# A two-layer conditioned decoder trunk: the list scheduler orders its instructions with a timeline model of the machine

## The chip, the cores and the metric

The kernel runs on one core of a Trainium2 chip. The metric is the device time of one execution in microseconds (us), the median of three runs.

## What is computed

The reference is a trunk of two post-norm layers on one sequence of 256 tokens with 1024 features, in float32. Each layer has three sub-layers: a SwiGLU feed-forward network (FFN, inner width 2816), a mixer, and a second FFN. Layer 0 mixes with a gated linear recurrence (RG-LRU) and chunked gated linear attention side by side, layer 1 with multi-head latent attention. A conditioning vector `c` gives shift, scale and gate vectors for each sub-layer, and each sub-layer ends in a layer norm over the residual sum:

```
for l in range(DEPTH):
    mod = c_act @ mod_w[l] + mod_b[l]
    sh1, sc1, g1, sh2, sc2, g2, sh3, sc3, g3 = jnp.split(mod, N_MOD, axis=-1)
    f = swiglu(modulate(x, sh1, sc1), ffn_in[l, 0], ffn_out[l, 0])
    x = deepnorm_residual(x, f, g1, ln_g[l, 0], ln_b[l, 0], 0.5)
    u = modulate(x, sh2, sc2)
...
    x = deepnorm_residual(x, m, g2, ln_g[l, 1], ln_b[l, 1])
    f = swiglu(modulate(x, sh3, sc3), ffn_in[l, 1], ffn_out[l, 1])
    x = deepnorm_residual(x, f, g3, ln_g[l, 2], ln_b[l, 2], 0.5)
```

Here `deepnorm_residual` is `layer_norm(DN_ALPHA * x + weight * (1 + gate) * f)`, and `m` is the mixer's output.

## The kernel before

**Layout.** Activations are kept transposed: features on the 128 partitions, the 256 tokens on the free axis, so that a vector of 1024 features is 8 tiles of 128x256. A weight block of 128x128 is loaded into TensorE (PE) and a tile of activations is streamed past it.

**Weights.** The weights arrive in the order in which they are used, as slabs of 1 MB (16 blocks), by transfers that SyncE (SP) issues into the buffers `wraw`. To keep float32 accuracy each half slab is split in two parts: ScalarE (ACT) makes the high part `whi` at L354, VectorE (DVE) the low part `wlo` at L355, five buffers each. The activations are split in the same way into `uhi` and `ulo` (or `hhi` and `hlo` inside an FFN). Each block then takes three matmuls: L432 (high by high), L433 (low activations by high weights) and L434 (high activations by low weights), in `mm3`.

**Modulation.** The matrix `mod_w` comes in slabs too, through the same `wraw` buffers and the same SP queue. DVE reduces 144 of its blocks with the conditioning vector (L406). A table of targets sets how many reduces are due at each slab of weights; they are spread over the whole kernel, ahead of where their vectors are needed.

**An FFN.** In `ffn`, the first passes go over groups of output tiles with the feature tile k outside, so that they need `u(k)` one by one. ACT applies SiLU, DVE multiplies (L772), and the product is split by ACT (L479) and DVE (L480). Where the first passes cover only part of the features, ACT keeps the partial sums and DVE adds them at L817. Then come the output matmuls.

**A boundary between sub-layers** (class `Boundary`). DVE makes the residual sum of each output tile at L648, adds to running sums (L655, L656), and scales the unnormalised tile into `flat` (ACT L620, DVE L621). Behind the last tile, `stats` runs four matmuls with a matrix of ones: L664 and L666 sum to the mean, L665 and L667 to the mean of squares. ACT squares the mean (L675), DVE takes the variance (L681) and subtracts the mean from each of the 8 tiles (L670, `center`), and `rsqrt2` gives the inverse deviation `r` (ACT L454, DVE L756 and L757). While that goes on, PE runs "early" matmuls: the first blocks of the next sub-layer's weights on the unnormalised tiles, whose result is corrected afterwards (ACT L707, DVE L709 and L710). They are 48 matmuls at the boundary that the prediction shows, accumulators `mm_4864` and `mm_4904`. `u(k)` then gives the normalised, modulated tile: DVE L725 makes `ut`, ACT L728 the high part `uhi`, DVE L729 the low part `ulo`. `residual` makes the input of the next residual sum: DVE L735 (`xh`, three buffers) and ACT L736, 8 of each; it is needed only at the end of the sub-layer.

**What sets the order.** The code above is a program in source order. The tile framework's list scheduler turns it into one queue for each engine, which the engine then runs strictly in order; semaphores make an instruction wait for its operands and its buffers. The scheduler picks among the instructions that it holds to be ready by priority. The code raises priorities (`tc.high_priority`, with an offset of 100 for `u(k)`, of 60 for the corrections of the early tiles, and the default for the boundary), fixes the order of a few stretches (`tc.manual_schedule`), and adds edges without semaphores between single instructions (`queue_behind`). What it holds to be ready, and when, is its model's matter.

The function that the change touches:

## Time and profile before

| quantity | value |
|---|---|
| runs (us) | 1019.43, 1019.33, 1018.88; median 1019.33 |
| profiled execution (us) | 1018.88, its span 1017.2 |
| PE, DVE, ACT busy (us) | 996.6, 876.8, 611.4 |
| DMA | 258.56 MB, mean 254 GB/s |
| granted PE clock, mean | 0.997 |

A busy time is the time in which an engine has an instruction in work. An engine's line in the timeline gives the start, the duration, the engine, the source line, the operation, the tiles (result on the left of the arrow) and their shape; a bracket behind it tells how long the engine was idle just before, and what it waited for. Durations overlap: an engine takes the next instruction before the last one has ended, so the price of an instruction in a full queue is the distance from its start to the next start.

### The profile page before, as it was taken

What the parts mean: (1) busy time and instruction counts of PE and PEld (TensorE: products, weight loads), DVE (VectorE), ACT (ScalarE), POOL (GpSimd) and SP (SyncE); (2) the same over time, 40 slices, a digit from 0 to 9 for tenths busy, and PEclk for the clock granted to TensorE, in tenths of its full rate; (3) what the DMA queues carried; (4) which work ended last, traced back from release to release, by engine and by line L of the source; (5) the groups of instructions that cost most, each with busy time, mean ns of one, the idle gap of its engine ahead of it and who ended that gap; (6) DMA issues with size and microseconds to landing.
All of it is one profiled execution on the core that took longest, in us unless ns stands there. A gap on an engine that the chain in (4) does not pass through costs nothing.

```text
span 1017.2 us, 20534 instructions
## 1 busy us (share of the span) xinstructions
PE 996.6 (98%) x8344; PEld 976.4 (96%) x8344; DVE 876.8 (86%) x1503; ACT 611.4 (60%) x1021; POOL 6.7 (1%) x27
## 2 busy tenths in 40 slices
PE   9999999999999999999999999999999999999995
PEld 7999999998999999999999999999999899999995
DVE  5789999798999999999987899999788799667664
ACT  4756665578896766655555664454568776454542
POOL 0000000000000000000000000000000000000000
PEclk9999999999999999999999999999999999999998
DMA  9997798554467954799986479898743146766501
GB/s 346 417 380 297 279 354 319 223 203 174 159 252 297 355 198 172 273 375 398 338 296 246 166 261 385 325 338 320 277 166 125 54 178 237 268 225 242 193 16 42
DMA packets 38145, 258.56 MB, mean 254 GB/s; under 512 B 4241, under 2 KB 5777, under 8 KB 7714
## 3 DMA queue, kind: packets, MB, share of 16 engines
q1 hardware_dynamic: 38050, 257.25, 67.4%
q8 instruction: 65, 1.06, 0.4%
q14 instruction: 30, 0.25, 0.1%
HBM read 256.18 MB, written 1.05 MB: 253 GB/s over the span
## 4 chain that ended last, share of the span: by engine, by line
PE 81%; DVE 15%; issue 2%; ACT 2%; DMA 1%; DVEq 0%; ACTq 0%
PE mm L433 23%; PE mm L432 23%; PE mm L434 23%; DVE wlo L355 5%; DVE junk L406 3%; PE mm L795 2%; PE mm L1074 1%; PE mm L1073 1%; DMA wraw<-modw 1%; PE mm L1075 1%; PE ax L795 1%; DVE flat L817 0%; DVE flat L941 0%; DVE ax L636 0%; DVE h L772 0%
## 5 line engine op out<-in xcount | busy, mean ns | idle before, releaser
L355 DVE TENSOR_TENSOR wlo<-wraw,whi 128x1024 fp32r<-128x1024 f32 x338 | 411.5, 1225 | 74.6 <-ACT whi L354 74.2
L354 ACT ACTIVATE whi<-wraw 128x1024 fp32r<-128x1024 f32 x338 | 355.4, 1058 | 186.2 <-PE mm L433 147.7
L432 PE MATMUL mm<-uhi,whi 128*128 128x256 f32 x1624 | 449.2, 277 | 1.3 <-ACT sg L454 1.3
L433 PE MATMUL mm<-ulo,whi 128*128 128x256 f32 x1624 | 449.5, 277 | 0.2 <-DVE ulo L729 0.2
L434 PE MATMUL mm<-uhi,wlo 128*128 128x256 f32 x1624 | 449.2, 277 | 0.0
L432 PEld LDWEIGHTS mm<-uhi,whi 128*128 128x128 f32 x1624 | 304.4, 188 | 1.7 <-ACT sg L454 1.5
L433 PEld LDWEIGHTS mm<-ulo,whi 128*128 128x128 f32 x1624 | 305.0, 188 | 0.7 <-DVE ulo L729 0.4
L434 PEld LDWEIGHTS mm<-uhi,wlo 128*128 128x128 f32 x1624 | 305.0, 188 | 0.1
L434 PE MATMUL mm<-hhi,wlo 128*128 128x256 f32 x704 | 194.7, 277 | 1.1 <-DVE wlo L355 1.1
L433 PE MATMUL mm<-hlo,whi 128*128 128x256 f32 x704 | 194.6, 276 | 0.0
L432 PE MATMUL mm<-hhi,whi 128*128 128x256 f32 x704 | 194.6, 276 | 0.0
L406 DVE CUSTOM_DVE_ANT_0 junk<-wraw,cact,cols 128x1024 bf16<-128x1024 f32 x136 | 174.9, 1286 | 7.9 <-DMA wraw<-modw 7.0
L434 PEld LDWEIGHTS mm<-hhi,wlo 128*128 128x128 f32 x704 | 132.2, 188 | 1.3 <-DVE wlo L355 1.3
L433 PEld LDWEIGHTS mm<-hlo,whi 128*128 128x128 f32 x704 | 132.2, 188 | 0.0
L432 PEld LDWEIGHTS mm<-hhi,whi 128*128 128x128 f32 x704 | 132.2, 188 | 0.0
L479 ACT ACTIVATE hhi<-h 128x256 fp32r<-128x256 f32 x88 | 35.7, 414 | 60.2 <-DVE h L772 60.0
L652 ACT ACTIVATE ysq<-yy 128x256 f32<-128x256 f32 x42 | 17.5, 416 | 43.8 <-DVE yy L648 41.0
L772 DVE SCALAR_TENSOR_TENSOR h<-mm,sg 128x256 f32<-128x256 f32 x75 | 31.6, 427 | 7.8 <-PE mm L434 7.5
L480 DVE TENSOR_TENSOR hlo<-h,hhi 128x256 fp32r<-128x256 f32 x88 | 36.7, 426 | 0.2 <-ACT hhi L479 0.2
L648 DVE SCALAR_TENSOR_TENSOR yy<-mm,gate,ax 128x256 f32<-128x256 f32 x48 | 23.2, 482 | 15.2 <-PE mm L434 15.2
L454 ACT ACTIVATE sg<-mm 128x256 f32<-128x256 f32 x75 | 27.4, 367 | 6.8 <-PE mm L434 4.8
L432 PE MATMUL mm<-flat,whi 128*128 128x258 f32 x96 | 28.5, 297 | 0.0
(310 smaller groups left out, 1117.5 us busy)
## 6 DMA issues: line engine op xcount, KB each, us to landing
wraw<-wst SPq DMA_DIRECT2D x165, 1024.0 KB, 5.6
wraw<-modw SPq DMA_DIRECT2D x71, 1024.0 KB, 7.1
wraw<-wst SPq DMA_DIRECT2D x10, 512.0 KB, 9.9
wraw<-modw SPq DMA_DIRECT2D x2, 512.0 KB, 5.3
yy<-xT SPq DMA_DIRECT2D x8, 128.0 KB, 10.2
wraw<-rgw SPq DMA_DIRECT2D x1, 1024.0 KB, 4.8
outT<-yy SPq DMA_DIRECT2D x3, 256.0 KB, 2.5
outT<-yy SPq DMA_DIRECT2D x2, 128.0 KB, 2.1
```

The lines of the kernel that those rows point to most:

```text
L354: ia = act.activation(hi, raw, AF.Copy)
L355: i = vec.tensor_tensor(lo, raw, hi.bitcast(F32), SUB)
L406: i = vec.tensor_tensor_reduce(junk, t, cact, 1.0, bias, MULT, ADD, self.modcols[(l, v)][:, j:j + 1])
L432: pe.matmul(ps, hi, mh, start=start, stop=False, skip_group_check=shared)
L433: pe.matmul(ps, hi, ml, start=False, stop=False, skip_group_check=shared)
L434: pe.matmul(ps, lo, mh, start=False, stop=stop, skip_group_check=shared)
L454: i = act.activation(out, in_, func, **kw)
L479: act.activation(hi, src, AF.Copy)
L480: return vec.tensor_tensor(lo, src, hi.bitcast(F32), SUB)
L648: vec.scalar_tensor_tensor(y, ps, self.gate[:, f:f + 1], ax[:, f, :], MULT, ADD)
L772: vec.scalar_tensor_tensor(h, pu, bu, sg, ADD, MULT)
L795: pe.matmul(grp[j][:, half * SEQ:(half + 1) * SEQ], wt[w], mv, start=k == ks[0] and half == 0 and t == 0, stop=k == ks[-1] and t == len(te ...
```

## The change

One argument is given to the context in which the program is recorded:

```
-    with _tile.TileContext(nc) as tc:
+    with _tile.TileContext(nc, schedule_with_timeline_sim=True) as tc:
         trunk_kernel(tc, *args)
```

With it the scheduler decides by a timeline model of the machine, and no longer by its plain one, when an instruction is ready and which comes next. The sources of the operations, their priorities, the fixed stretches and the added edges stay. The same instructions come out, in another order: 1345 lines of the order differ on PE, 1956 on DVE, 1033 on ACT, 24 on SP and 11 on GpSimd.

Here is what DVE's queue holds at the end of layer 0's mixer, behind the statistics. `v_4843` is the variance, `yy_4208` the 8 residual sums, `ut_4860` and `ut_4987` belong to `u(0)` and `u(1)`, and `wlo` are low parts of weights. Before:

```order
L681 TENSOR_TENSOR v_4843<-ax_4836,v_4843 128x256
L670 TENSOR_TENSOR yy_4208<-yy_4208,ax_4835 128x256 x4
L756 SCALAR_TENSOR_TENSOR t_4853<-v_4843,t_4853 128x256
L670 TENSOR_TENSOR yy_4208<-yy_4208,ax_4835 128x256
L757 SCALAR_TENSOR_TENSOR r_4852<-t_4853,r_4852 128x256
L670 TENSOR_TENSOR yy_4208<-yy_4208,ax_4835 128x256
L725 SCALAR_TENSOR_TENSOR ut_4860<-yy_4208,hA_4231,r_4852 128x256
L709 SCALAR_TENSOR_TENSOR early_4901<-mean_4845,wab_4899,mm_4864 128x256
L725 SCALAR_TENSOR_TENSOR ut_4987<-yy_4208,hA_4231,r_4852 128x256
L729 SCALAR_TENSOR_TENSOR ulo_138<-ut_4860,B_4223,uhi_137 128x256
```

Now DVE's queue has, from L681 on, all eight L670, two L709, L756, L757, and two each of L725 and L710, and then these rows, in which `junk` is a modulation reduce and `xh` a residual step:

```order
L355 TENSOR_TENSOR wlo_4868<-wraw_4576,whi_4867 128x1024
L355 TENSOR_TENSOR wlo_4872<-wraw_4576,whi_4871 128x1024
L355 TENSOR_TENSOR wlo_4910<-wraw_4662,whi_4909 128x1024
L355 TENSOR_TENSOR wlo_4960<-wraw_4662,whi_4959 128x1024
L406 ISA junk_5136,mod_8_817_5135<-wraw_4905,cact_96,cols_97 128x1024
L406 ISA mod_8_817_5135 128x1
L735 SCALAR_TENSOR_TENSOR xh_5262<-yy_4208,ag_4227,r_4852 128x256
L735 SCALAR_TENSOR_TENSOR xh_5265<-yy_4208,ag_4227,r_4852 128x256
L735 SCALAR_TENSOR_TENSOR xh_5268<-yy_4208,ag_4227,r_4852 128x256
L729 SCALAR_TENSOR_TENSOR ulo_138<-ut_4860,B_4223,uhi_137 128x256
```

The first L729 has moved from the 12th instruction behind L681 to the 26th (repeats and the read of the accumulator counted), behind four weight conversions, a reduce and three residual steps.

On PE at the same place, the statistics stood ahead of the early matmuls, whose first blocks follow. `mm_4864` is an early accumulator:

```order
L664 MATMUL ax_4835<-acc_4209,ones_dm_98 128x256
L665 MATMUL ax_4836<-acc_4209,ones_dm_98 128x256
L666 MATMUL ax_4835<-yy_4208,ones_dm_98 128x256
L432 MATMUL mm_4864<-flat_692_4233,whi_4699 128x258
L667 MATMUL ax_4836<-ysq_4831,ones_dm_98 128x256
L433 MATMUL mm_4864<-flat_693_4234,whi_4699 128x258
L434 MATMUL mm_4864<-flat_692_4233,wlo_4700 128x258
```

Now they stand behind the early matmuls, and the first matmuls on `u(0)`, with accumulators `mm_4955` to `mm_4958`, follow at once:

```order
L434 MATMUL mm_4864<-flat_692_4233,wlo_4700 128x258
L433 MATMUL mm_4904<-flat_693_4234,whi_4736 128x258
L434 MATMUL mm_4904<-flat_692_4233,wlo_4737 128x258
L664 MATMUL ax_4835<-acc_4209,ones_dm_98 128x256
L666 MATMUL ax_4835<-yy_4208,ones_dm_98 128x256
L665 MATMUL ax_4836<-acc_4209,ones_dm_98 128x256
L667 MATMUL ax_4836<-ysq_4831,ones_dm_98 128x256
L432 MATMUL mm_4955<-uhi_137,whi_4802 128x256
L432 MATMUL mm_4956<-uhi_137,whi_4802 128x256
L432 MATMUL mm_4957<-uhi_137,whi_4802 128x256
L432 MATMUL mm_4958<-uhi_137,whi_4802 128x256
L433 MATMUL mm_4955<-ulo_138,whi_4802 128x256
```

The last early matmul has moved from some 5.5 us of PE work behind L667 to ahead of it, and the first L432 on `u(0)` from behind the early matmuls to right behind L667.

At the end of layer 0, on the way to the first FFN of layer 1, DVE's queue now holds this around the first two `ulo` (`ut_7259` and `ut_7379` are those of `u(0)` and `u(1)`):

```order
L725 SCALAR_TENSOR_TENSOR ut_7259<-yy_6486,hA_6497,r_7251 128x256
L710 SCALAR_TENSOR_TENSOR early_7294<-early_7294,r_7251 128x256
L725 SCALAR_TENSOR_TENSOR ut_7379<-yy_6486,hA_6497,r_7251 128x256
L355 TENSOR_TENSOR wlo_7352<-wraw_7075,whi_7351 128x1024
L709 SCALAR_TENSOR_TENSOR early_7332<-mean_7244,wab_7330,mm_7297 128x256
L735 SCALAR_TENSOR_TENSOR xh_7653<-yy_6486,ag_6493,r_7251 128x256
L735 SCALAR_TENSOR_TENSOR xh_7656<-yy_6486,ag_6493,r_7251 128x256
L735 SCALAR_TENSOR_TENSOR xh_7659<-yy_6486,ag_6493,r_7251 128x256
L406 ISA junk_7529,mod_3_1089_6816<-wraw_7298,cact_96,cols_97 128x1024
L406 ISA mod_3_1089_6816 128x1
L504 TENSOR_SCALAR v_8876<-v_8876,cols_97 128x256
L729 SCALAR_TENSOR_TENSOR ulo_138<-ut_7259,B_6489,uhi_137 128x256
```

In before, that first L729 stands behind L681 with five L670, L756, L757, one L355, two L725 and one L709 between; now residual steps, two reduces and three L355 stand there as well.

## Prediction

> **What bounds the kernel now.** I read the page first: its head, the busy times, the chain that ended last.

> ```profile
> span 1017.2 us, 20534 instructions
> PE 996.6 (98%) x8344; PEld 976.4 (96%) x8344; DVE 876.8 (86%) x1503; ACT 611.4 (60%) x1021; POOL 6.7 (1%) x27
> PE 81%; DVE 15%; issue 2%; ACT 2%; DMA 1%; DVEq 0%; ACTq 0%
> ```

> PE has work in 98% of the span, and the chain runs through it for 81% and through DVE for 15%. So the kernel has almost no slack on PE, and any new PE idle time is paid in full, while DVE at 86% can hide a reordering only where it has a lead. How tight that is, the waits of PE tell (us in total, times, longest):

> ```profile
> PE ax L1130 <- DVE B L601: 1.7, 1, 1.7
> PE mm L432 <- ACT sg L454: 1.3, 1, 1.3
> PE mm L434 <- DVE wlo L355: 1.1, 1, 1.1
> PE mm L433 <- DVE ulo L729: 0.2, 1, 0.2
> ```

> The largest single wait is 1.7 us, and the matmuls that need the low part of the normalised activations (ulo, L729) wait 0.2 us in the whole run. That last row is the one that the change will move. Next I read the timeline at one sub-layer boundary, from the mixer of layer 0 to its second FFN. PE first (start, us, engine, line, operation):

> ```profile
> 375.78 0.28 PE L432 MATMUL mm<-uhi,whi 128*128 128x256 f32 x1
> ...
> 380.43 0.28 PE L434 MATMUL mm<-uhi,wlo 128*128 128x256 f32 x1
> ...
> 382.24 0.60 PE L667 MATMUL ax<-ysq,ones_dm 128*128 128x256 f32 x2
> ...
> 388.31 0.28 PE L432 MATMUL mm<-uhi,whi 128*128 128x256 f32 x1
> ```

> The first two rows are 41 matmuls apart: 4.65 us, so 0.1133 us from start to start. That is the price of a matmul here. L667 finishes the statistics at 382.84. The first matmul that needs the normalised activations (L432 on uhi) starts at 388.31. In the 5.5 us between, PE runs the early matmuls on the unnormalised activations (flat), without a gap. DVE in the same time:

> ```profile
> 382.94 0.42 DVE L681 TENSOR_TENSOR v<-ax,v 128x256 f32<-128x256 f32 x1
> 383.28 1.41 DVE L670 TENSOR_TENSOR yy<-yy,ax 128x256 f32<-128x256 f32 x4
> ...
> 385.93 0.48 DVE L725 SCALAR_TENSOR_TENSOR ut<-yy,hA,r 128x256 f32<-128x256 f32 x1
> 386.83 0.48 DVE L709 SCALAR_TENSOR_TENSOR early<-mean,wab,mm 128x256 f32<-128x256 f32 x1 [0.41 <-ACT wab L707]
> 387.23 0.48 DVE L725 SCALAR_TENSOR_TENSOR ut<-yy,hA,r 128x256 f32<-128x256 f32 x1
> 387.62 0.48 DVE L729 SCALAR_TENSOR_TENSOR ulo<-ut,B,uhi 128x256 fp32r<-128x256 f32 x1
> 388.02 0.42 DVE L710 SCALAR_TENSOR_TENSOR early<-early,r 128x256 f32<-128x256 f32 x1
> 388.35 0.48 DVE L729 SCALAR_TENSOR_TENSOR ulo<-ut,B,uhi 128x256 fp32r<-128x256 f32 x1
> 388.75 2.35 DVE L355 TENSOR_TENSOR wlo<-wraw,whi 128x1024 fp32r<-128x1024 f32 x2
> 391.02 0.48 DVE L709 SCALAR_TENSOR_TENSOR early<-mean,wab,mm 128x256 f32<-128x256 f32 x1
> ```

> L681 starts 0.10 us after L667's end and the first ulo is done at 388.10, 0.3 us ahead of its matmul: the early matmuls cover this chain almost exactly. The same rows price DVE's work, from start to start. L681 is 0.34. The eight operations from 383.28 to 385.93 (six L670, L756, L757) are 0.33 each, L710 too. L709, L725 and L729 are 0.40, and L355 is 1.135 (two in 2.27). Further prices, from later in the same FFN:

> ```profile
> 405.84 1.28 DVE L406 CUSTOM_DVE_ANT_0 junk<-wraw,cact,cols 128x1024 bf16<-128x1024 f32 x1
> 407.04 0.08 DVE L406 DVE_READ_ACCUMULATOR2_ANT mod<- 128x1 f32 x1
> ...
> 409.38 0.48 DVE L735 SCALAR_TENSOR_TENSOR xh<-yy,ag,r 128x256 f32<-128x256 f32 x1
> 409.78 0.42 DVE L772 SCALAR_TENSOR_TENSOR h<-mm,sg 128x256 f32<-128x256 f32 x1
> 410.12 1.22 DVE L355 TENSOR_TENSOR wlo<-wraw,whi 128x1024 fp32r<-128x1024 f32 x1
> ...
> 411.58 0.42 DVE L480 TENSOR_TENSOR hlo<-h,hhi 128x256 fp32r<-128x256 f32 x1
> 411.91 1.28 DVE L406 CUSTOM_DVE_ANT_0 junk<-wraw,cact,cols 128x1024 bf16<-128x1024 f32 x1
> ```

> So a modulation reduce (L406) is 1.20, a residual step (L735) 0.40, L772 and L480 0.33 each. In before, the first L735 of this FFN runs at 409.38 and the first reduce at 405.84, more than 20 us behind the statistics.

> **The change part by part.** No instruction is added or removed; each engine runs the same work in another order. In order queues that costs nothing except where a loop closes: a PE instruction that DVE waits for, a block of DVE work queued behind it, and a later PE instruction that waits for the end of that block. If the DVE block is longer than the PE work between the two, PE must idle for the difference, whatever else happens. I looked for such blocks along the two orders, with the prices above. The waits that they give in before are those that the rows of waits show; after has seven of another size.

> *Boundaries.* The new order places the statistics L664 to L667 behind the early matmuls, so that L432/L433 on u follow L667 at once: the cover of 5.5 us is gone, since it now lies ahead of the chain and not beside it. And DVE's queue ahead of ulo is longer: all eight L670, residual steps L735, reduces L406 and weight conversions L355 stand there. At the boundary shown above, DVE has from L681 to the fifth L729: L681 0.34, 8 L670 2.64, L756 and L757 0.66, 2 L709 0.80, 6 L725 2.40, 2 L710 0.66, 7 L355 7.95, 5 L406 6.00, 8 L735 3.20, 5 L729 2.00, L772, L480 and two small ones 0.80. The sum is 27.45. Between L667 and the L433 that waits for that L729, PE has 102 matmuls, 11.56. The difference, 15.9, is PE idle time; 13 of it comes at the first L433. The other boundaries by the same prices:
> - layer 0, first FFN to mixer: 8 L670, 3 L355, 2 L709, 2 L725 and five others, 9.4, against 30 matmuls, 3.4: 6.0.
> - layer 0 to layer 1: 8 L670, 6 L355, 6 L406, 8 L735, 6 L725, 5 L729 and others with 1.6 of rope tables, 29.0, against 128 matmuls, 14.5: 14.5.
> - layer 1, first FFN to attention: 8 L670, 8 L735, 5 L355, 4 L709, 4 L710 and others, 16.5, against 74 matmuls and three of two passes, 9.7: 6.8.
> - layer 1, attention to second FFN: 8 L670, 8 L735, 3 L355, 2 L406, 4 L725, 3 L729 and others, 16.8, against 52 matmuls, 5.9: 10.9.

> Together 54.1. Before waits a few tenths at each (0.2 at ulo, above); less 0.3 each, 1.5, that is 52.6.

> *Two long blocks.* In the first FFN and in layer 0's mixer DVE is full already. Windows of before (us, PE busy, PEld, DVE, ACT, POOL, clock, DMA share, GB/s):

> ```profile
> 97.00:142.00 45.00, 43.69 (x385) 43.49 (x385) 45.00 (x78) 31.03 (x49) 0.00 (x0) 1.00 0.84 315
> ...
> 259.00:303.00 44.00, 42.94 (x328) 41.04 (x328) 42.98 (x70) 38.00 (x77) 0.00 (x0) 1.00 0.56 207
> ```

> The timeline prices what else is in the mixer's block, the chain what is in the FFN's:

> ```profile
> 258.44 0.69 DVE L932 TENSOR_SCALAR ya<-ya 128x1024 f32<-128x1024 f32 x1
> 259.04 0.48 DVE L735 SCALAR_TENSOR_TENSOR xh<-yy,ag,r 128x256 f32<-128x256 f32 x1
> 259.44 1.22 DVE L933 SCALAR_TENSOR_TENSOR ya<-ya,ya 128x1024 f32<-128x1024 f32 x1
> 260.57 0.42 DVE L1055 TENSOR_TENSOR bc<-bc,mm 128x256 f32<-128x256 f32 x1
> ...
> 267.51 2.44 DVE L941 TENSOR_TENSOR_SCAN flat<-ya,ya 128x256 f32<-128x256 f32 x4
> ```

> ```profile
> 104.61 0.60 DVE flat L817
> ```

> In the first FFN 16 L355, 15 L406, 14 L772, 14 L480 and 7 L817 (0.60) now lie in one loop: 18.2 + 18.0 + 4.6 + 4.6 + 4.2 and 0.3 of small ones are 49.9. Its 390 matmuls take 45.6 at the window's own pace (385 in 45.0): 4.3 more. In the mixer 12 L406, 12 L355, 12 L921 (0.40, an operation of L725's kind and size), 6 L735, 4 L941 (0.61), four wide ones of 1.13 and two of 0.60, with 5.1 of small ones, come to 48.5 against the 44.0 that the window took for nearly the same PE work: 4.5 more.

> *Smaller terms.* The first FFN's block also needs a modulation slab whose transfer is now queued behind a conversion that ends 4.2 us before its reduce.

> ```profile
> wraw<-modw SPq DMA_DIRECT2D x71, 1024.0 KB, 7.1
> ```

> By the median landing that is 7.1 − 4.2 = 2.9 more, between 0 and 7. Two ACT conversions (L354, 1.06 by the group's mean) now stand ahead of ACT's part of the statistics at two boundaries: between 0 and 2.1 each, and I take 0.7, since ACT had idle time just ahead; 1.4. ACT's tanh chain in the mixer closes a loop 1.4 longer than DVE's. Seven loops each cross from PE to DVE and back; the crossing above took 0.10, and I take 0.3 for both ways with ACT between: 2.1. Four transfers of 128 KB move forward at the head, where the matmuls of the first FFN follow their slab within a microsecond: 0 to 3, taken as 1. Together 8.8.

> *PE's clock.* Before has no PE pause long enough to show what a pause does, except after its last matmul:

> ```profile
> 1005.26 0.65 PE L667 MATMUL ax<-ysq,ones_dm 128*128 128x256 f32 x2
> ```

> ```profile
> 1008.00:1012.00 4.00, 0.00 (x0) 0.00 (x0) 3.44 (x9) 2.40 (x5) 0.30 (x1) 0.89 0.08 30
> 1012.00:1016.00 4.00, 0.00 (x0) 0.00 (x0) 1.66 (x5) 0.87 (x2) 0.00 (x0) 0.50 0.66 234
> ```

> The granted clock (third from the end) is 0.50 from 1012 and 0.89 in the 4 us before: if it went from 1 to 0.5 in one step, that was 0.9 us before 1012, some 5.2 us after the last matmul's end at 1005.9. The five boundary waits reach or pass that. How long the clock stays down on return no row shows. If as long as it took to fall, each such wait costs half of 5.2, 2.6, and five cost 13; where further waits for DVE follow at once, the slower matmuls hide in them, down to 0. I take three waits (the two of 15 and that of 11) at 1.3: 4. [...]

> Sum: 52.6 + 4.3 + 4.5 + 8.8 + 4 = 74.2 on the profiled execution's own time, 1018.88 (span 1017.2), which is the fastest of the three runs and 0.45 below their median. That gives 1093.

> **The rivals.**
> - *The waits are partly paid back.* While PE waits, DMA and ACT run ahead, and the waits that before has elsewhere (the rows of waits above, and such as these) fall away: 1.7 + 1.3 + 1.1, so 4.1 less; the small terms are then hidden too, 8.8, and the clock costs nothing, 4. That gives 1076. For it speaks that DVE has 140 us of idle time in the span. Against it: waits close a loop, and the idle time lies elsewhere.
> - *The clock and the transfers charge in full.* All five boundaries at 2.6 (9 more than taken), and three further reduces queued less than 7.1 us behind their slab's issue, some 4 each: 1114.
> - *Faster.* The new PE order runs the high terms (L432) of four tiles before the first low one, so that a late ulo or wlo stops less. If the waits of before vanish and no new ones come, 1018.9 − 4.1 = 1014.8. It decides at the first L433 behind L667: four L432, 0.45 us, are all that PE has there, and DVE would have to reach ulo in that time; by its queue it needs 13. For it speaks only that reading the queue order could mislead where DVE has nothing to wait for; against it, that the engines run in order.
> - *Nothing moves in time.* Were the order only shuffled among instructions with slack, no change. Against it are rows that put 20 us of DVE work between the statistics and the first ulo.

> **How the numbers follow.** The forecast has 0.72, the first rival 0.12, the second 0.11, faster 0.03, nothing 0.02. The low end takes the first rival's 1076 and a miscounted loop of 6 besides, 1070; the high end takes 1114 and as much on the other side, 1120. A measurement of this kernel can tell some 0.2%, 2 us, from no change; both outer cases with no slower time together have 0.05, so slower has 0.95.

> **What would show it.** In the profile of the changed kernel PE should be busy near 91 to 93% of the span, and "PE mm L433 <- DVE ulo L729" should rise from 0.2 us to some 40 in a handful of waits, the longest 11 to 14, at the boundaries behind L667. The time between L667 and the first L433 on ulo at layer 0's last boundary should be about 13, with L735 and L406 run in it. The granted clock should dip there. Busy times of DVE and ACT stay as they are. It is wrong if DVE's queue reaches ulo within a microsecond or two of L667, or if the added time lies outside these seven places, such as in waits for slabs; and a time under 1070 would mean that loops overlap.

## The result, and the profile after

The changed kernel takes 1118.26 us (median of six runs, 1113.37 to 1124.60) against 1019.25 of the kernel before on the same chip: a ratio of 1.097, 95% interval 1.095 to 1.100. The forecast was 1093, with a range to 1120; the median lies 1.7 us under that upper end, and two of the six runs (1124.06 and 1124.60) lie above it. The profiled execution of after took 1124.06, of which the span is 1122.3; it is 105.2 longer than that of before.

The page of after first: span, busy times, the chain.

```profile
span 1122.3 us, 20553 instructions
PE 1025.2 (91%) x8344; PEld 997.5 (89%) x8344; DVE 882.1 (79%) x1503; ACT 612.9 (55%) x1021; POOL 6.7 (1%) x27
PE 65%; DVE 14%; DMA 12%; issue 5%; ACT 3%; SPq 0%; DVEq 0%; ACTq 0%
PE mm L433 20%; PE mm L434 20%; PE mm L432 19%; DMA wraw<-modw 11%; DVE wlo L355 4%; DVE junk L406 4%; DVE yy L670 1%; DVE xh L735 1%; ACT whi L354 1%; PE mm L1075 1%; PE mm L1074 1%; PE mm L1073 1%; DMA wraw<-wst 1%; DVE h L772 1%; PE ax L434 0%
```

DVE and ACT do the same work in the same time as before. PE has fallen from 98% to 91% of a longer span, but two things here were not foreseen in this size. PE's busy time has grown by 28.6 us with not one matmul more. That is the clock: by their starts and ends, the matmuls that start while the granted clock is 0.50 are busy some 27 us longer than at the pace of before. And the chain now runs through transfers of modulation slabs (modw) for 11% of the span, where before had 1% for them. The waits of PE (in total, times, longest):

```profile
PE mm L432 <- ACT uhi L728: 24.9, 4, 8.3
PE mm L433 <- DVE ulo L729: 12.9, 5, 6.6
PE mm L432 <- ACT sg L454: 8.0, 1, 8.0
PE ax L631 <- ACT shift L629: 6.8, 2, 4.5
PE ax L1177 <- ACT sg L1176: 5.0, 2, 4.9
```

The first two rows are the waits at the boundaries: 37.8 together, where before had 0.2. Next the boundary that the prediction worked out, on DVE and then on PE:

```profile
412.08 0.42 DVE L681 TENSOR_TENSOR v<-ax,v 128x256 f32<-128x256 f32 x1 [3.34 <-ACT v L675]
...
417.90 0.42 DVE L710 SCALAR_TENSOR_TENSOR early<-early,r 128x256 f32<-128x256 f32 x1
418.23 4.62 DVE L355 TENSOR_TENSOR wlo<-wraw,whi 128x1024 fp32r<-128x1024 f32 x4
422.77 1.28 DVE L406 CUSTOM_DVE_ANT_0 junk<-wraw,cact,cols 128x1024 bf16<-128x1024 f32 x1
423.98 0.08 DVE L406 DVE_READ_ACCUMULATOR2_ANT mod<- 128x1 f32 x1
423.98 1.27 DVE L735 SCALAR_TENSOR_TENSOR xh<-yy,ag,r 128x256 f32<-128x256 f32 x3
425.17 0.48 DVE L729 SCALAR_TENSOR_TENSOR ulo<-ut,B,uhi 128x256 fp32r<-128x256 f32 x1
```

```profile
411.11 0.59 PE L667 MATMUL ax<-ysq,ones_dm 128*128 128x256 f32 x2
417.84 1.22 PE L432 MATMUL mm<-uhi,whi 128*128 128x256 f32 x4 [6.14 <-ACT uhi L728]
425.70 0.58 PE L433 MATMUL mm<-ulo,whi 128*128 128x256 f32 x1 [6.63 <-DVE ulo L729]
```

DVE runs the queue that the order showed: from L681 at 412.08 to the first L729 at 425.17 are 13.1 us, as forecast (12.8 by the prices). PE pays it in two waits of 6.14 and 6.63, with four L432 between. In before, early matmuls lay beside the chain to both; here L432 waits for `uhi`, whose `ut` stands behind all eight L670. Four conversions (4.54), one reduce and three residual steps (2.40) then separate `ut` from `ulo`.

To see where the 105 us lie I cut both traces at the same amounts of PE work (each matmul counted at its own price, 0.113 us for 256 columns) and took the time that passed above it in each stretch. Us added by the change, beside what the prediction's terms give for that place:

| place (time in before) | added | forecast |
|---|---|---|
| first FFN, around L817 (108 to 150) | 8.6 | 7.2 |
| layer 0, first FFN to mixer (191 to 233) | 7.3 | 5.7 |
| layer 0's mixer (275 to 317) | 11.0 | 5.9 |
| mixer to second FFN (380 to 421) | 16.3 | 16.3 |
| second FFN of layer 0, its middle (502 to 522) | 11.4 | 0 |
| layer 0 to layer 1 (562 to 603) | 14.9 | 14.2 |
| first FFN of layer 1, its end (664 to 704) | 11.6 | 0 |
| layer 1, first FFN to attention (744 to 766) | 8.8 | 6.5 |
| attention (766 to 811) | 4.7 | 0 |
| attention to second FFN (811 to 852) | 13.9 | 11.3 |
| everywhere else | -3.3 | clock, crossings and head 7.1 |

The seven places of the forecast have 80.8 of the 105.2; the rows of the two FFNs are what it missed. Here is the one in layer 0: SP's issue of a modulation slab, then DVE, then PE.

```profile
551.90 0.33 SPq L389 DMA_DIRECT2D wraw<-modw  x1
```

```profile
550.59 1.28 DVE L406 CUSTOM_DVE_ANT_0 junk<-wraw,cact,cols 128x1024 bf16<-128x1024 f32 x1
...
559.17 1.28 DVE L406 CUSTOM_DVE_ANT_0 junk<-wraw,cact,cols 128x1024 bf16<-128x1024 f32 x1 [4.29 <-DMA wraw<-modw]
...
562.73 0.48 DVE L648 SCALAR_TENSOR_TENSOR yy<-mm,gate,ax 128x256 f32<-128x256 f32 x1
```

```profile
558.92 0.28 PE L432 MATMUL mm<-hhi,whi 128*128 128x256 f32 x1
563.71 0.58 PE L631 MATMUL ax<-shift,ones_r 128*128 128x256 f32 x1 [4.51 <-ACT shift L629]
564.09 0.42 PE L433 MATMUL mm<-hlo,whi 128*128 128x256 f32 x1
...
569.42 0.36 PE L434 MATMUL mm<-hhi,wlo 128*128 128x256 f32 x1
```

A reduce ends at 551.87 and frees its buffer; SP issues the next slab at 551.90; it lands 7.25 us later, and DVE, with little else ahead of the slab's own reduce, waits 4.29 of it. Behind that reduce in DVE's queue stands L648, the first output tile's sum, on which `shift` and PE's L631 hang. This is a loop between DVE and the transfer, turn after turn: DVE's waits for modulation slabs are 55.4 us in after, 7.0 in before. PE has a lead at first and pays when it is used up.

The last rows show the clock too. From 564.09 to 569.42 are 25 matmuls, 0.213 us apart and not 0.113, until the pace comes back; the granted clock in 564 to 568 is 0.50.

### The profile page after: what moved, and what is told of

Its sections match the earlier page's. It is cut to its first block, busy times and chain, and to the rows that moved or that the text cites. A ratio compares the mean times of both kernels' runs of the same rounds, so it can differ in the third digit from the quotient of the medians.

```text
span 1122.3 us, 20553 instructions
## 1 busy us (share of the span) xinstructions
PE 1025.2 (91%) x8344; PEld 997.5 (89%) x8344; DVE 882.1 (79%) x1503; ACT 612.9 (55%) x1021; POOL 6.7 (1%) x27
## 3 DMA queue, kind: packets, MB, share of 16 engines
q8 instruction: 65, 1.06, 0.4%
## 4 chain that ended last, share of the span: by engine, by line
PE 65%; DVE 14%; DMA 12%; issue 5%; ACT 3%; SPq 0%; DVEq 0%; ACTq 0%
PE mm L433 20%; PE mm L434 20%; PE mm L432 19%; DMA wraw<-modw 11%; DVE wlo L355 4%; DVE junk L406 4%; DVE yy L670 1%; DVE xh L735 1%; ACT whi L354 1%; PE mm L1075 1%; PE mm L1074 1%; PE mm L1073 1%; DMA wraw<-wst 1%; DVE h L772 1%; PE ax L434 0%
## 5 line engine op out<-in xcount | busy, mean ns | idle before, releaser
L354 ACT ACTIVATE whi<-wraw 128x1024 fp32r<-128x1024 f32 x338 | 356.5, 1059 | 263.7 <-PE mm L433 210.5
L355 DVE TENSOR_TENSOR wlo<-wraw,whi 128x1024 fp32r<-128x1024 f32 x338 | 411.0, 1222 | 105.1 <-ACT whi L354 102.5
L432 PE MATMUL mm<-uhi,whi 128*128 128x256 f32 x1624 | 448.8, 281 | 36.0 <-ACT uhi L728 24.9
L433 PE MATMUL mm<-ulo,whi 128*128 128x256 f32 x1624 | 453.1, 280 | 13.0 <-DVE ulo L729 12.9
L434 PE MATMUL mm<-uhi,wlo 128*128 128x256 f32 x1624 | 450.3, 280 | 0.9 <-DVE wlo L355 0.9
L432 PEld LDWEIGHTS mm<-uhi,whi 128*128 128x128 f32 x1624 | 307.8, 191 | 38.3 <-ACT uhi L728 26.1
L433 PEld LDWEIGHTS mm<-ulo,whi 128*128 128x128 f32 x1624 | 310.6, 191 | 14.6 <-DVE ulo L729 14.6
L434 PEld LDWEIGHTS mm<-uhi,wlo 128*128 128x128 f32 x1624 | 309.3, 191 | 1.2 <-DVE wlo L355 1.1
L406 DVE CUSTOM_DVE_ANT_0 junk<-wraw,cact,cols 128x1024 bf16<-128x1024 f32 x136 | 174.4, 1282 | 56.1 <-DMA wraw<-modw 55.4
L432 PE MATMUL mm<-hhi,whi 128*128 128x256 f32 x704 | 197.1, 280 | 4.1 <-ACT hhi L479 4.1
L433 PE MATMUL mm<-hlo,whi 128*128 128x256 f32 x704 | 197.4, 280 | 1.3 <-DVE hlo L480 1.3
L434 PE MATMUL mm<-hhi,wlo 128*128 128x256 f32 x704 | 197.4, 280 | 1.2 <-DVE wlo L355 1.2
L432 PEld LDWEIGHTS mm<-hhi,whi 128*128 128x128 f32 x704 | 134.9, 192 | 4.5 <-ACT hhi L479 4.5
L433 PEld LDWEIGHTS mm<-hlo,whi 128*128 128x128 f32 x704 | 135.0, 192 | 1.9 <-DVE hlo L480 1.7
L434 PEld LDWEIGHTS mm<-hhi,wlo 128*128 128x128 f32 x704 | 134.9, 192 | 1.6 <-DVE wlo L355 1.6
L479 ACT ACTIVATE hhi<-h 128x256 fp32r<-128x256 f32 x88 | 36.3, 413 | 99.5 <-DVE h L772 99.2
L648 DVE SCALAR_TENSOR_TENSOR yy<-mm,gate,ax 128x256 f32<-128x256 f32 x48 | 22.8, 480 | 20.3 <-PE mm L434 20.3
L772 DVE SCALAR_TENSOR_TENSOR h<-mm,sg 128x256 f32<-128x256 f32 x75 | 30.9, 420 | 8.6 <-PE mm L434 7.0
L480 DVE TENSOR_TENSOR hlo<-h,hhi 128x256 fp32r<-128x256 f32 x88 | 36.2, 420 | 0.0
L454 ACT ACTIVATE sg<-mm 128x256 f32<-128x256 f32 x75 | 27.6, 367 | 7.7 <-DVE h L772 4.4
## 6 DMA issues: line engine op xcount, KB each, us to landing
wraw<-wst SPq DMA_DIRECT2D x165, 1024.0 KB, 5.2
wraw<-modw SPq DMA_DIRECT2D x71, 1024.0 KB, 5.6
wraw<-rgw SPq DMA_DIRECT2D x1, 1024.0 KB, 4.8
```

The costliest lines, as they stand in the source:

```text
L354: ia = act.activation(hi, raw, AF.Copy)
L355: i = vec.tensor_tensor(lo, raw, hi.bitcast(F32), SUB)
L406: i = vec.tensor_tensor_reduce(junk, t, cact, 1.0, bias, MULT, ADD, self.modcols[(l, v)][:, j:j + 1])
L432: pe.matmul(ps, hi, mh, start=start, stop=False, skip_group_check=shared)
L433: pe.matmul(ps, hi, ml, start=False, stop=False, skip_group_check=shared)
L434: pe.matmul(ps, lo, mh, start=False, stop=stop, skip_group_check=shared)
```

## The experiments

Most of them hold single engines to their former order. A scratch program is scheduled as before, and its order on an engine is laid on the program with edges that only order, without semaphores; the timeline model orders the rest:

```
for row in held:
    row = [traced[n] for n in row if n in traced]
    for a, b in zip(row, row[1:]):
        tc.add_manual_dep(b, a.name, mybir.DependencyInfo(
            mybir.DependencyClass.NoSync, mybir.DependencyReason.DATA), reason="order")
...
plain = build(False)
nc = build(True, [order(plain, DVE)])
```

Holding one engine also moves the others, since the model arranges them around it. By operation, tile and shape, e1 has another matmul than the changed kernel at 2234 of the 8344 places of PE's queue, and e9 at 2027. So each run prices an engine's order together with the model's answer to it, and places added below are read from one profiled execution of each run.

The theories, as they are called below: Q, DVE's queue ahead of `ulo` makes the waits; P, PE's own order does; S, SP issues the slabs too late.

**e1, DVE as before** (`order(plain, DVE)`).

> DVE is held to the order that it had before; PE, ACT, SP and GpSimd are ordered by the timeline model as in the changed kernel. Theory Q (the order in DVE's queue ahead of ulo makes the waits): the reduces and residual steps no longer stand ahead of ulo, and only the missing cover is left, some 4 to 5 us at each of five boundaries (the chain from L681 to the first ulo took 5.2 us before), so 20 to 30 us with the clock that falls there: 1040 to 1055, and the two waits of about 11 us in the middle of FFNs, where DVE stood waiting for a modulation slab, are gone. Theory P (PE's own order costs the time): it stays over 1090. Theory S (SP issues the slabs too late): the two waits in the FFNs stay, and the time is about 20 us above Q's, 1062 to 1075.

Measured: 1079.94, ratio 1.059 (1.058 to 1.061). DVE's order is worth 38 us, the most of any engine. The two waits in the FFNs are gone (0.0 us added at both places), DVE's waits for slabs are back at 9.9, and S falls. But 61 us are left, more than Q gave. At the boundary of the prediction 7.3 are left, and at the last one 14.3.

**e2, PE as before** (`order(plain, PE)`).

> PE is held to the order that it had before, with the statistics ahead of the early matmuls; the other engines are ordered by the timeline model. Theory Q: the early matmuls cover up to 5.4 us of DVE's chain again at each of five boundaries, but ulo still stands behind residual steps, reduces and conversions: waits of some 13, 13, 7 and 3 us stay, the FFNs still wait for slabs; 1080 to 1095. Theory P: 1019 to 1030. Theory S: close to Q, it doesn't tell the two apart.

Measured: 1106.33, ratio 1.085 (1.082 to 1.087). PE's order by itself gives back 12 us: P falls, and Q took too much for the cover.

**e3, PE and DVE as before** (`order(plain, PE), order(plain, DVE)`).

> PE and DVE are both held to the order that they had before; ACT, SP and GpSimd are ordered by the timeline model. Theory Q: nothing is left but small changes on ACT and SP: 1018 to 1026. A theory by which ACT's order (conversions of weights ahead of the statistics) or SP's costs time of its own: over 1030.

Measured: 1045.87, ratio 1.025 (1.023 to 1.028). Q fails here: 27 us are left with both engines in order, and they are ACT's or SP's. A wait of 2.07, the fourth of its waits by size, shows one way. ACT, then PE, at the end of a pass of the first FFN:

```profile
121.11 1.06 ACT L354 ACTIVATE whi<-wraw 128x1024 fp32r<-128x1024 f32 x1 [2.43 <-DMA wraw<-wst]
122.08 0.40 ACT L454 ACTIVATE sg<-flat 128x256 f32<-128x256 f32 x1
122.39 0.36 ACT L454 ACTIVATE sg<-mm 128x256 f32<-128x256 f32 x1
```

```profile
122.80 0.39 PE L432 MATMUL mm<-uhi,whi 128*128 128x256 f32 x1 [2.07 <-ACT sg L454]
```

A weight conversion (L354) stands ahead of the SiLUs and waits for its slab, and the SiLUs wait with it, though what they need is there; PE waits for the accumulator that the SiLU frees.

**e4, SP as before** (`order(plain, mybir.EngineType.SP)`).

> SP is held to the order that it had before; the other engines are ordered by the timeline model. Theory Q: the boundaries are as in the changed kernel, and the slabs are late because a buffer comes free late and not because of the order of the issues: 1110 to 1125. Theory S: the two waits of about 11 us in the FFNs vanish, 1090 to 1100.

Measured: 1112.76, ratio 1.091 (1.087 to 1.095); the runs (1106 to 1116) overlap with those of the changed kernel. DVE's waits for slabs are still 44.2, and the FFN's two places still add 6.6 each, so SP's order is not what makes these waits. Whether it has a part in the 10 us by which the two places fell, or the spread of the runs has, was not separated.

**e5, only SP and GpSimd by the timeline model** (PE, DVE and ACT held).

> PE, DVE and ACT are held to the order that they had before; only SP and GpSimd are ordered by the timeline model. If ACT's order made the 27 us by which the kernel with PE and DVE held is above the one before, nothing is left here: 1018 to 1023. If SP's order made them, it stays at 1040 to 1048.

Measured: 1021.06, ratio 1.0013 (1.0003 to 1.0022). So the 25 us between e3 and here are ACT's order.

**e6, statistics ahead of the early matmuls.** `mm3` returns its first matmul:

```
+            last_sum = pe.matmul(e2, ones_dm, ysq, start=False, stop=True)
...
+                    queue_behind(mm3(...), last_sum)
```

> The changed kernel, with one edge more at each boundary: the first early matmul of each early tile is queued behind the last statistics matmul (L667), as PE had them before. Theory Q by the loops of this order: DVE's and ACT's queues are nearly unchanged, and the early matmuls lie beside DVE's chain again; the summed loops fall by 19 us (between 15 and 25), to 1093 to 1104. If the place of the statistics is the whole of it: under 1060. If it is of no matter, since the DVE queue is long anyway: over 1110.

Measured: 1107.04, ratio 1.086 (1.083 to 1.089), 11 us gained, and by place the reason isn't the one expected. At the five boundaries together only 2 us are gone; most of the gain lies in the two FFN waits for slabs (1.0 and 6.5 added, before this edit 11.4 and 11.6), though DVE's queue in layer 0's FFN is the same row for row from 491 us to the wait at 559 (ahead of 491 rows had changed places). So what PE pays at such a place hangs on the timing with which it gets there. Why the boundaries gain so little, PE's row at the statistics of one of two such boundaries shows:

```profile
408.09 1.19 PE L664 MATMUL ax<-acc,ones_dm 128*128 128x256 f32 x2 [4.23 <-DVE acc L655]
```

Now PE waits ahead of the statistics, for running sums that DVE makes late. In the changed kernel the early matmuls cover that wait; moved back, they cover the one behind.

**e7, reduces and conversions in their former relative order.** Only L355 and L406 are held, among themselves.

> The changed kernel, but DVE's weight conversions (L355) and modulation reduces (L406) keep, among themselves, the relative order that they had before; all else is ordered by the timeline model. Theory Q: no reduce stands ahead of ulo, the long blocks of the first FFN and of layer 0's mixer lose 10 us, the boundaries 12, and the two waits of about 11 us for slabs in the FFNs go: 1065 to 1080. If the reduces are of no matter: over 1105.

Measured: 1089.07, ratio 1.068 (1.066 to 1.069), 29 us gained; the time lies above Q's range. The FFN waits add 0.0, the mixer 3.9 and not 11.0, layer 0 to layer 1 9.4 and not 14.9; DVE's waits for slabs are 5.7. The first FFN's place stays at 8.9, against what was expected: three conversions in a row still stand ahead of an L772 there. With all of DVE held that place adds 3.9 (e1), with ACT held as well 0.5 (e9), so both engines' orders make it; which rows of them was not settled.

**e8, residual steps behind the last ulo.**

```
+                i = vec.scalar_tensor_tensor(xg, ..., MULT, MULT); self.done and queue_behind(i, self.last_u)
```

> The changed kernel, but the residual steps (L735) are queued behind the last ulo (L729) of their sub-layer. Theory Q: 8 steps of 0.40 us leave the way to ulo at three boundaries, and come back behind it, where they delay L772 at two of them; the summed loops fall by 8 us: 1104 to 1114. If the residual steps are the main weight ahead of ulo: under 1090.

Measured: 1103.49, ratio 1.081 (1.079 to 1.083), 15 us gained. Three boundaries lose 2.2, 2.8 and 2.0, so 7 of the 8 that the loops gave; the time lies half a microsecond under Q's range. The two FFN places lose 16 besides, and the mixer takes 4 back.

**e9, DVE and ACT as before**, so PE's order is left.

> DVE and ACT are held to the order that they had before; PE, SP and GpSimd are ordered by the timeline model, so this is the price of PE's order by itself. If the place of the statistics matters once DVE and ACT are in order: the chain from L681 to the first ulo (5.2 us before) lies open at five boundaries, less a tenth or two of other work, and each such wait brings the clock down: 20 to 35 us, so 1039 to 1054. If PE's order is harmless when the other two are in order: 1019 to 1026.

Measured: 1062.51, ratio 1.043 (1.041 to 1.044): the place of the statistics does matter once the others are in order, but the range was too low. The boundary of the prediction shows what was expected:

```profile
407.35 1.22 PE L432 MATMUL mm<-uhi,whi 128*128 128x256 f32 x4 [3.68 <-ACT uhi L728]
```

The five boundaries add 1.7, 6.3, 2.1, 3.6 and 9.3, so 23; the mixer 8.1 and attention 4.9, since PE's order reaches into them, and that I had left out.

**e10, ACT as before**, the others by the timeline model.

> ACT is held to the order that it had before; PE, DVE, SP and GpSimd are ordered by the timeline model. With PE and DVE in order, ACT's order cost 25 us. If that adds to what the others cost: 1088 to 1098. If ACT's delays mostly lie beside waits for DVE at the same places: 1104 to 1118.

Measured: 1113.38, ratio 1.092 (1.090 to 1.095). Worth 25 with the others in order, ACT's order is worth 5 without. The 5 is a balance: in the profiled execution the two FFN places fall from 23.0 to 2.4 and the five boundaries by 6, while the other places add 18, with PE's waits for `whi` up from 1.2 to 8.2. So it is not shown that ACT's delays lie beside those of DVE.

**e11, the edits of e6, e7 and e8 together.**

> The changed kernel with the three single edits together: statistics ahead of the early matmuls, reduces and conversions in their former relative order, residual steps behind the last ulo. The single edits gave 11, 29 and 15 us. If they add up: 1060 to 1068. If the edits open each other (the statistics' place was worth little because ulo was late anyway): 1045 to 1058. If they overlap: over 1070.

Measured: 1069.59, ratio 1.050 (1.048 to 1.051). The three gave 55 singly and 49 together, nearly a sum, but by place it is none. The five boundaries lose 2, 7 and 7 in the single runs and 28 together: there the edits open each other, as the second theory had it. The two FFN places lose 16, 23 and 16 singly and 23 together, since that time can go only once. Some 50 us stay in the rest of the order.

**e12, one trait of the new order on the old kernel.** With the plain scheduler, L434 of up to four blocks is held back behind L432 and L433 of all of them.

```
+        ...; late.append((ps, lo, mh, stop, shared))
+        ...; now = late[:] if stop or len(late) == LATE else []
+        [pe.matmul(ps, lo, mh, ...) for ps, lo, mh, stop, shared in now]; del late[:len(now)]
```

> The kernel before, with its plain scheduler, and one trait of the new order alone: the low-weight matmuls (L434) of four blocks follow the high ones (L432, L433) of all four. If that trait helps by itself, the waits for wlo go (1.1 us and a few tenths): 1017 to 1019, 0.1 to 0.2% under before. If not: 1019 to 1022.

Measured: 1018.76, ratio 1.000 (0.999 to 1.001): no difference that can be told. PE's wait for `wlo` fell from 1.1 to 0.8. No version here beats the kernel before.

The engines in one table, each row with those engines held to the former order:

| held | median us | over before |
|---|---|---|
| none | 1118.3 | 99 |
| ACT | 1113.4 | 94 |
| SP | 1112.8 | 93 |
| PE | 1106.3 | 87 |
| DVE | 1079.9 | 61 |
| DVE, ACT | 1062.5 | 43 |
| PE, DVE | 1045.9 | 27 |
| PE, DVE, ACT | 1021.1 | 2 |

## Why the prediction was right, and where it was not

- *The direction and the mechanism hold.* The loops between DVE and PE at the boundaries were counted at 54.1 and are there, in place and nearly in size: 61.2 added with the crossings, ACT's part and the clock in it, against 54.0 with only the ACT terms. e1 shows that DVE's order is the largest part. At the boundary shown, PE takes 14.0 from L667 to the first L433 on `ulo`, where about 13 was said. But 23.0 in waits for slabs and 4.7 in attention lie outside the seven places, which the prediction had named as a sign against itself.
- *"The first FFN's block also needs a modulation slab ... 2.9 more" was the step that failed.* It weighed slabs at one place only, by one queue position, and there PE did not pay: DVE waits 2.5 for a slab at 146.0, and PE's only long wait in that FFN, 7.98, ends before it, at 125.73. So the 8.6 against 7.2 there agrees by luck: holding DVE takes 4.7 of it away (e1; 4.3 was the price of its block), and holding ACT as well takes 3.4 more (e9). In the FFNs the new order spaces the reduces so that each slab is issued when the reduce before it ends, and needed sooner than it lands. That costs 23.0 at two places with a forecast of 0; it was in the rival with 1114, at 12. e1 and e7 remove it, e4 does not. DVE's waits for these slabs follow the order of its reduces: 4.0 to 9.9 us in the six runs that keep this order as before, wholly or nearly (e1, e3, e5, e7, e9, e11), and 36.3 to 55.4 in the changed kernel and the five that do not (e2, e4, e6, e8, e10). What PE pays of them at the two places varies more, from 23.0 to 13.2 (e4), 7.5 (e6), 7.0 (e8) and 2.4 (e10), and what sets that stays open.
- *"Two ACT conversions ... 1.4" and "tanh chain ... 1.4" looked for ACT's part at three places.* With PE and DVE in order it is 25 (e3 against e5), and little of it lies there: the two boundaries add 0.5 and 2.3 in e3, the mixer 0.5. What it costs in the changed kernel stays open (e10). The mixer, forecast 5.9, added 11.0; e7 brings that to 3.9 and e10 leaves 12.6, so ACT's chain is not what makes the excess, and DVE's order is not alone in it, since e1 still adds some 9. Attention added 4.7 that no term had.
- *"The cover of 5.5 us is gone" holds, but not as a price that can be had back.* e6 shows the same matmuls covering another wait of 4.2; only with DVE and ACT in order is the cover worth 23 (e9).
- *The clock was sized too low.* Taken as 4, it cost some 15 in eight unbroken stretches of 12 to 25 matmuls 0.21 us apart, by their starts in the trace. The prediction took three falls; the granted clock fell eleven times ahead of the last matmul. The rest of the 27 us lies on matmuls between waits, and how much of it lengthened the run is not shown.
- *The waits split.* The sign "L433 <- ulo some 40, the longest 11 to 14" did not come out: 12.9 for `ulo`, 24.9 for `uhi`, with the longest at 8.3, because `ut` itself comes late.
- *The range held by little, and that was luck.* The sum gave 74, the median shows 99. The upper end stood on the rival with 1114, which charged 13 for the clock and 12 more for slabs; its parts are the nearer ones.
- The profiled execution's gap to the forecast, 31, is thus 23.0 in the FFNs, 4.7 in attention, 7.6 at the seven places above their terms with clock and crossings (73.2), less 4.3 elsewhere, where waits of before fell away, as the first rival had it (4.1), and the head cost nothing.

The other rivals fell by the result: the faster one needed DVE at the first `ulo` in 0.45 us, and it took 13.1.

## What to carry to other kernels

Where all queues run in order, read a new schedule by its loops: what an engine waits for, the block that is queued behind it, and who waits for the end of that block. Count those loops through every engine and through the transfers, because the next slab's issue hangs on the same queue. Low-urgency work (reduces, residual steps, conversions) ahead of a short chain on which the busiest engine hangs costs most of its length there (in e8, 2.0 to 2.8 us of the 3.2 of eight residual steps), even if the engine that runs it idles elsewhere. Compare single edits by place and not by their totals alone: in e10 and e11 gains and losses at different places cancel. And holding one engine's order does not leave the others' as they were.

## What the runs showed of the hardware

A short PE wait cost a second time: in e3 one of 2.07 us was enough (windows: us, PE, PEld, DVE, ACT, POOL busy, granted clock, DMA share, GB/s):

```profile
120.00:124.00 4.00, 1.93 (x13) 1.74 (x12) 4.00 (x9) 2.58 (x7) 0.00 (x0) 0.89 0.88 303
124.00:128.00 4.00, 4.00 (x27) 4.00 (x26) 2.95 (x6) 0.97 (x3) 0.00 (x0) 0.68 0.87 367
128.00:132.00 4.00, 4.00 (x38) 4.00 (x37) 3.10 (x5) 2.77 (x6) 0.00 (x0) 1.00 0.46 160
```

In 124 to 128 PE ran 27 matmuls in the time of 38, though it was busy throughout. In the changed kernel one such stretch cost 1.2 to 2.5 us. The fall, at 123.13, came 2.4 us behind the start of the wait, sooner than the 5.2 us that the end of before's trace had suggested, and here it followed a wait that the prediction would have taken to be free of it.

The runs of the changed kernel spread more than those of before: its six lie within 1.0%, the others within 0.25%. Among the variants of the changed kernel, those with 36 us or more of slab waits spread by 0.33 to 0.9%, those with under 10 by 0.23 to 0.35%. That the transfers are the cause is not shown.
